# Gate and up products of two feed-forwards as seven block products of half the rows and half the tokens

## The chip, the cores and the metric

The kernel runs on one core of one Trainium2 chip. The metric is the device time of one execution in microseconds (us). Three runs of the kernel before gave 1549.69, 1547.15 and 1549.71 us, with a median of 1549.69. The engines are named TensorE (PE in the rows), VectorE (DVE), ScalarE (ACT), GpSimd (POOL) and SyncE (SP), which here only issues the transfers of weights.

## The reference, cut to what matters

Two transformer blocks follow each other on 512 tokens of width 1024. The first block has a feed-forward, a mixer (attention and pooling) and a second feed-forward; the change concerns its two feed-forwards. All arithmetic is float32.

```python
def rmsnorm(x, g):
    xf = x.astype(jnp.float32)
    y = xf * lax.rsqrt(jnp.mean(xf * xf, axis=-1, keepdims=True) + EPS)
    return (y * g.astype(jnp.float32)).astype(x.dtype)

def swiglu_ffn(x, w_gate, w_up, w_down):          # 1024 -> 2816 -> 1024
    return (jax.nn.silu(x @ w_gate) * (x @ w_up)) @ w_down

def first_block(x, ...):
    x = x + 0.5 * swiglu_ffn(rmsnorm(x, ffn1_norm[l]), ffn1_w_gate[l], ffn1_w_up[l], ffn1_w_down[l])
    x = x + hybrid_mixer(rmsnorm(x, mix_norm[l]), w_in[l], ...)
    x = x + 0.5 * swiglu_ffn(rmsnorm(x, ffn2_norm[l]), ffn2_w_gate[l], ffn2_w_up[l], ffn2_w_down[l])
    return rmsnorm(x, final_norm[l])
...
    x = second_block(x, ...)
```

## The kernel before

Activations lie transposed in SBUF: a tile is 128 features by 512 tokens, and x has eight of them (KD = 8, S = 512, H2 = 256). Every float32 product is made of three products on TensorE in a shorter format (fp32r). Each operand is split into a high part and the remainder: `split` rounds on ScalarE (`whi`, `xh`) and subtracts on VectorE (`wlo`, `xl`), and `mm3` adds high times high, high times low and low times high in one PSUM bank.

A feed-forward (`ffn`) takes the 2816 inner columns in three chunks of 8, 8 and 6 tiles of 128 (`FF1_CHUNKS`). For a pair, which is one tile of gate and one of up, `fgroup` makes 8 x 3 matmuls of 512 columns for gate and as many for up. The normalising factor of a token (`rsb`) is applied afterwards: VectorE multiplies both results by it out of PSUM, ScalarE makes silu of gate, GpSimd multiplies by up, and `split` makes the two parts of the inner activation (tiles `hh` and `hl` in the arena; a1f and a1r, or a2f and a2r, in the rows). After the pairs of a chunk come eight groups of down products, each added to X by VectorE.

Weights come in pieces of 1024 columns of 128 partitions (512 KB) by SyncE's queue into the ring `wraw` (three buffers), and `w_pump` splits each into the rings `whi` and `wlo` (four), two pieces ahead of their use (`SPLIT_AHEAD`).

Before the first feed-forward, `first_norm` transposes x in eight steps, splits it with its gain into `xh` and `xl`, copies it to X, and sums its squares (`sq` on ScalarE, `acc` on GpSimd). The second feed-forward's operands are prepared by `prep_sq` as the mixer's last products arrive. Small rows (gains, biases) are loaded by GpSimd's queue in the first microseconds (tile `rows`), and the mixer's Toeplitz table (`toeplitz`, held in XT) beside the first feed-forward.

The order of the instructions on each engine is written by a planner. Class `Program` collects all operations with a price for each (`cost`: by engine, columns, and whether PSUM is read; 2.11 ns a column + 147 ns for a tensor_tensor on GpSimd, 1.041 + 69 on VectorE with two operands) and a delay for a signal between engines; `issue` tries several sweeps, keeps the order that ends first, and issues it as a fixed order for each engine. Engines then wait for each other through semaphores only. There are two plannings: the first feed-forward and the mixer (arena a1), then the second feed-forward and the second block (arena a2). All recorded instructions have the line of that issue, so a row is told apart by its tiles.

Of the kernel before, what the change touches and what calls it, by code (L numbers as in the profile page):

```python
# [24 lines left out]
R_BUFS = 3  # L25
SPLIT_AHEAD = 2
ARENA = (5500, 16050)
# [250 lines left out]
class Arena:  # L278
# [13 lines left out]
    def tile(self, shape, dt=F32):  # L292
        n = math.prod(shape[1:])
        whole, at = self.whole[dt], self.at[dt]
        assert at + n <= whole.shape[1], (shape, dt, at)
        ap = whole[:shape[0], at:at + n]
        self.at[dt] += n
# [17 lines left out]
class Kern:  # L315
# [6 lines left out]
    def mm(self, out, lhsT, rhs, start=True, stop=True):  # L322
        self.pe.matmul(out, lhsT=lhsT, rhs=rhs, start=start, stop=stop)
# [107 lines left out]
    def w_init(self, pool):  # L431
        self.L = self.plan()
        self.raw = [pool.tile([P, 1024], F32, name=f"wraw{i}") for i in range(R_BUFS)]
        self.wh = [pool.tile([P, 1024], F32R, name=f"whi{i}") for i in range(W_BUFS)]
        self.wl = [pool.tile([P, 1024], F32R, name=f"wlo{i}") for i in range(W_BUFS)]
        self.w_dma = self.w_split = self.w_cur = 0
# [11 lines left out]
    def w_pump(self, upto):  # L448
        while self.w_split < min(upto + 1, len(self.L)):
            i = self.w_split  # L450
            self.w_load(i + R_BUFS)
            m = self.L[i][2] * self.L[i][3]
            step = m // 2 if i < 2 else m
            for c in range(0, m, step):
                c = slice(c, c + step)
                self.split(self.wh[i % W_BUFS][:, c], self.wl[i % W_BUFS][:, c], self.raw[i % R_BUFS][:, c])
            self.w_split += 1
            self.w_load(self.w_split + R_BUFS)

    def W(self, key, ahead=SPLIT_AHEAD):  # L460
        i = self.w_cur
        assert self.L[i][0] == key, (self.L[i][0], key)
        self.w_pump(i + ahead)
        self.w_cur += 1
        return self.w_view(self.wh[i % W_BUFS], i), self.w_view(self.wl[i % W_BUFS], i)


    def mm3(self, ps, ah, al, bh, bl, start, stop):
        self.mm(ps, ah, bh, start, False)
        self.mm(ps, ah, bl, False, False)  # L470
        self.mm(ps, al, bh, False, stop)
# [9 lines left out]
    def fgroups(self, bs, ws, xs, cols=slice(0, S)):  # L481

        n = len(xs)
        for k in range(n):
            for b, (wh, wl) in zip(bs, ws):
                self.mm3(b, wh[:, k, :], wl[:, k, :], xs[k][0][:, cols], xs[k][1][:, cols], k == 0, k == n - 1)

# [42 lines left out]
    def prep_sq(self, m, gcol):  # L530
        self.split(*self.xs[m], self.X[:, m, :], gcol)
        self.sq_acc(m, self.acc, self.X[:, m, :])
# [88 lines left out]
    def first_norm(self):  # L621
# [7 lines left out]
        self.w_pump(1)  # L629
# [780 lines left out]
```

## Time and profile before

| | |
|---|---|
| median of three runs | 1549.69 us |
| the profiled execution's own time | 1547.03 us |
| its span, first to last instruction | 1545.2 us |
| mean granted TensorE clock | 0.996 |
| TensorE busy | 1525.7 us (99%) |
| VectorE busy | 824.6 us (53%) |
| ScalarE busy | 648.4 us (42%) |
| GpSimd busy | 297.7 us (19%) |

A busy time is the time in which an engine has an instruction under way; the chain is the work that ended last, followed back from the end of the program. The rows that follow come from this one execution. A row of the timeline with xN stands for N like instructions in a row, with their time together.

### The profile page before, as it was taken

How to read it: one execution, taken by the hardware profiler on the slowest of the kernel's cores; microseconds unless marked ns; L12 is line 12 of the kernel's file. 1: busy time of each engine (PE TensorE's matmuls, PEld its weight loads, DVE VectorE, ACT ScalarE, POOL GpSimd, SP SyncE). 2: the span in 40 equal slices, each digit the busy share in tenths (PEclk: the TensorE clock that was granted, in tenths of full speed). 3: DMA queues.
4: the chain of work that ended last, by engine and by line, in shares of the span. 5: the costliest groups of instructions: out<-in, count | busy, mean ns of one | idle time of the engine just before them, and what ended most of it. 6: DMA issues, size and time to landing. Idle time of an engine off the chain costs nothing.

```text
span 1545.2 us, 18001 instructions
## 1 busy us (share of the span) xinstructions
PE 1525.7 (99%) x6931; PEld 1235.2 (80%) x6931; DVE 824.6 (53%) x1284; ACT 648.4 (42%) x1063; POOL 297.7 (19%) x290
## 2 busy tenths in 40 slices
PE   9999999999999999999999999999999999999997
PEld 7888888788877788888888887677788888888886
DVE  6443443336588884433443467998568524344345
ACT  6322232234367663312322275776555634233232
POOL 5120120212243321101200146331016000000002
PEclk9999999999999999999999999999999999999999
DMA  6333333533311133333433233121221332333321
GB/s 192 96 99 95 96 103 96 114 94 111 96 55 41 55 110 96 95 96 96 113 96 95 79 99 102 42 82 49 90 69 45 123 93 95 96 95 97 95 95 55
DMA packets 226757, 140.68 MB, mean 91 GB/s; under 512 B 5340, under 2 KB 212800, under 8 KB 226672
## 3 DMA queue, kind: packets, MB, share of 16 engines
q1 hardware_dynamic: 224832, 136.33, 30.1%
q0 software_dynamic: 1824, 3.21, 1.0%
q8 instruction: 54, 0.88, 0.2%
q14 instruction: 31, 0.25, 0.1%
q10 hardware_dynamic: 16, 0.00, 0.0%
HBM read 137.23 MB, written 2.29 MB: 90 GB/s over the span
## 4 chain that ended last, share of the span: by engine, by line
PE 92%; DVE 6%; ACT 1%; POOL 0%; issue 0%; DMA 0%; SPq 0%; DVEq 0%; POOLq 0%; ACTq 0%
PE bank L232 92%; DVE a2f L232 1%; DVE wlo L232 1%; ACT a2f L232 1%; DVE X L232 1%; DVE a2r L232 0%; DVE XT L232 0%; DVE xl L232 0%; DVE a1r L232 0%; DVE sq L232 0%; DMA XT<-x 0%; DVE cv L232 0%; POOL a2f L232 0%; DVE acc L232 0%; POOL acc L232 0%
## 5 line engine op out<-in xcount | busy, mean ns | idle before, releaser
L232 DVE TENSOR_TENSOR wlo<-wraw,whi 128x1024 fp32r<-128x1024 f32 (+2 forms) x258 | 325.2, 1262 | 417.8 <-ACT whi L232 352.9
L232 ACT ACTIVATE whi<-wraw 128x1024 fp32r<-128x1024 f32 (+2 forms) x258 | 267.5, 1039 | 518.8 <-PE bank L232 498.5
L232 PE MATMUL bank<-xl,whi 128*128 128x512 f32 (+1 forms) x1272 | 463.5, 384 | 2.5 <-DVE xl L232 2.5
L232 PE MATMUL bank<-xh,whi 128*128 128x512 f32 (+1 forms) x1272 | 462.6, 385 | 1.8 <-DVE a1r L232 1.0
L232 PE MATMUL bank<-xh,wlo 128*128 128x512 f32 (+1 forms) x1272 | 458.2, 383 | 0.0
L232 PEld LDWEIGHTS bank<-xl,whi 128*128 128x128 f32 x1272 | 239.4, 189 | 50.0 <-DVE xl L232 2.9
L232 PEld LDWEIGHTS bank<-xh,whi 128*128 128x128 f32 x1272 | 238.9, 189 | 49.7 <-issue 2.2
L232 PEld LDWEIGHTS bank<-xh,wlo 128*128 128x128 f32 x1272 | 239.1, 189 | 46.5 <-issue 1.9
L232 PE MATMUL bank<-whi,a2r 128*128 128x512 f32 (+1 forms) x528 | 155.6, 388 | 0.0
L232 PE MATMUL bank<-a1r,whi 128*128 128x512 f32 x480 | 151.2, 400 | 0.0
L232 PE MATMUL bank<-a2r,whi 128*128 128x512 f32 x416 | 130.0, 397 | 0.0
L232 POOL TENSOR_TENSOR a1f<-a1f 128x512 f32<-128x512 f32 x40 | 59.5, 1487 | 317.1 <-DVE a1f L232 311.6
L232 PEld LDWEIGHTS bank<-whi,a2r 128*128 128x128 f32 x528 | 98.2, 188 | 21.0
L232 POOL TENSOR_TENSOR a2f<-a2f 128x512 f32<-128x512 f32 x38 | 56.4, 1484 | 303.5 <-DVE a2f L232 252.3
L232 PEld LDWEIGHTS bank<-a1r,whi 128*128 128x128 f32 x480 | 89.7, 188 | 22.1 <-issue 0.9
L232 PE MATMUL bank<-wlo,a2r 128*128 128x512 f32 (+1 forms) x264 | 95.0, 389 | 0.0
L232 PEld LDWEIGHTS bank<-a2r,whi 128*128 128x128 f32 x416 | 77.3, 187 | 19.0 <-issue 0.7
L232 PE MATMUL bank<-a1r,wlo 128*128 128x512 f32 x240 | 91.1, 399 | 0.0
L232 ACT ACTIVATE a2r<-a2f 128x512 fp32r<-128x512 f32 (+3 forms) x83 | 51.0, 620 | 93.3 <-POOL a2f L232 55.3
L232 DVE TENSOR_TENSOR a2r<-a2f,a2r 128x512 fp32r<-128x512 f32 (+2 forms) x81 | 54.8, 680 | 49.7 <-ACT a2r L232 48.9
L232 PE MATMUL bank<-a2r,wlo 128*128 128x512 f32 x208 | 79.4, 397 | 0.0
L232 POOL TENSOR_TENSOR X<-X,a2f 128x512 f32<-128x512 f32 (+1 forms) x9 | 10.7, 1210 | 337.6 <-ACT a2f L232 337.6
(246 smaller groups left out, 1586.0 us busy)
## 6 DMA issues: line engine op xcount, KB each, us to landing
wraw<-ffn_w_gate SPq DMA_DIRECT2D x43, 512.0 KB, 3.8
wraw<-ffn_w_up SPq DMA_DIRECT2D x43, 512.0 KB, 3.8
wraw<-w_in SPq DMA_DIRECT2D x40, 512.0 KB, 3.9
wraw<-ffn_w_down SPq DMA_DIRECT2D x32, 512.0 KB, 3.9
wraw<-w_up SPq DMA_DIRECT2D x32, 512.0 KB, 4.0
wraw<-w_down SPq DMA_DIRECT2D x32, 512.0 KB, 3.6
wraw<-w_out SPq DMA_DIRECT2D x16, 512.0 KB, 3.5
wraw<-ffn_w_down SPq DMA_DIRECT2D x16, 384.0 KB, 3.4
```

The lines of the kernel that those rows point to most:

```text
L232: op.fn(*op.a, **op.k)
```

## The change

Two adjacent tiles of 128 columns, gate G and up U, over the 1024 rows of x form two by two blocks if the 1024 rows are halved (k tiles 0 to 3 and 4 to 7), and so does x, if the tokens are halved as well. The product needs eight block products in the plain way, which are the two groups of 24 matmuls before; the new `ffn` makes it of seven, each over four k steps and 256 tokens (`half_product`: 12 matmuls of 256 columns). The seven weights of a pair are three blocks, A11 and A12 (the two halves of gate) and A22 (the second half of up), and four sums S1 to S4 of blocks, made by GpSimd in the tiles sum0 and sum1; the seven operands of x are three blocks (11, 21, 22) and four differences (T1 to T4), made once for each feed-forward by `prep7` (ScalarE scales, VectorE and GpSimd subtract, and both parts are split). Weights are handled in units: `U` lists four for a pair (A11 and A12, S1 and S2, S3 and S4, A22) and one for a down group, and `W4` hands out a pair's four.

The seven results are combined while they are still in PSUM, partly by letting one bank accumulate two products and partly by VectorE (six additions or products of 256 columns out of PSUM, one of 256 from SBUF). The multiplication of up by `rsb` moves from VectorE to GpSimd. Scratch of the feed-forward moves into XT, so the Toeplitz table is loaded at the start of the mixer instead (`tape_out` and `toeplitz`). The second feed-forward moves to the first planning. The raw ring gets a fourth buffer. Of the diff, the new code is shown; what it takes the place of stands in the listing above.

```diff
--- before
+++ after
-R_BUFS = 3
+R_BUFS = 4
 SPLIT_AHEAD = 2
-ARENA = (5500, 16050)
+ARENA = (5640, 16050)
...
-        self.wh = [pool.tile([P, 1024], F32R, name=f"whi{i}") for i in range(W_BUFS)]
-        self.wl = [pool.tile([P, 1024], F32R, name=f"wlo{i}") for i in range(W_BUFS)]
-        self.w_dma = self.w_split = self.w_cur = 0
+        self.ring = [(pool.tile([P, 1024], F32R, name=f"whi{i}"), pool.tile([P, 1024], F32R, name=f"wlo{i}"))
+                     for i in range(W_BUFS)]
+        self.w_dma = self.w_made = self.w_cur = 0
+        self.U, self.at_unit = [], {}
+        for i, (key, _, _, _) in enumerate(self.L):
+            if key[1] == "u":
+                continue
+            self.at_unit[key] = len(self.U)
+            self.U += [(i, j) for j in range(4)] if key[1] == "g" else [(i, None)]
+        self.made = {}
+        self.sums = [pool.tile([P, 1024], F32, name=f"sum{q}") for q in range(2)]
...
+        while self.w_made < min(upto + 1, len(self.U)):
+            j = self.w_made
+            i, part = self.U[j]
+            h, l = buf = self.ring.pop(0)
+            self.ring.append(buf)
+            self.made[j] = buf
+            g = self.raw[i % R_BUFS]
+            if part is None:
+                self.w_load(i + 1)
+                m = self.L[i][2] * self.L[i][3]
+                self.split(h[:, :m], l[:, :m], g[:, :m])
+                self.w_load(i + 1 + R_BUFS)
+            else:
+                self.w_load(i + 2)
+                u = self.raw[(i + 1) % R_BUFS]
+                lo, hi = slice(0, S), slice(S, 2 * S)
+                if part == 0:
+                    for c in (lo, hi) if j < 4 else (slice(0, 2 * S),):
+                        self.split(h[:, c], l[:, c], g[:, c])
+                elif part == 3:
+                    self.split(h[:, lo], l[:, lo], u[:, hi])
+                    self.w_load(i + 2 + R_BUFS)
+                else:
+                    s12, s34 = self.sums
+                    if part == 1:
+                        self.tt(s12[:, lo], u[:, lo], u[:, hi], ALU.add, self.po)
+                        self.tt(s12[:, hi], s12[:, lo], g[:, lo], ALU.subtract, self.po)
+                        self.split(h, l, s12)
+                    else:
+                        self.tt(s34[:, lo], g[:, lo], u[:, lo], ALU.subtract, self.po)
+                        self.tt(s34[:, hi], g[:, hi], s12[:, hi], ALU.subtract, self.po)
+                        self.split(h, l, s34)
+            self.w_made += 1
...
+    def W4(self, key):
+        j = self.w_cur
+        assert self.at_unit[key] == j, (key, j)
+        self.w_pump(j + 3)
+        self.w_cur += 4
+        out = {}
+        for part, names in enumerate((("A11", "A12"), ("S1", "S2"), ("S3", "S4"), ("A22",))):
+            buf = self.made.pop(j + part)
+            for q, nm in enumerate(names):
+                out[nm] = tuple(t[:, q * S:(q + 1) * S].rearrange("p (k c) -> p k c", k=4) for t in buf)
+        return out
...
+    def half_product(self, ps, w, xs, start, stop):
+        wh, wl = w
+        for k in range(4):
+            self.mm3(ps, wh[:, k, :], wl[:, k, :], *xs[k], start and k == 0, stop and k == 3, skip_group_check=True)
...
+    def prep7(self, m, src, g):
+        hi, lo = self.mem7[m % 4]
+        st = self.first[m % 4]
+        b11, b12, t1 = (st[:, i * H2:(i + 1) * H2] for i in range(3))
+        if m < 4:
+            self.act(st[:, :2 * H2], src, AF.Copy, scale=g)
+            self.split(hi[:, :H2], lo[:, :H2], b11)
+            self.tt(t1, b12, b11, ALU.subtract, self.po)
+            self.split(hi[:, H2:2 * H2], lo[:, H2:2 * H2], t1)
+        else:
+            st = self.second.next()
+            b21, b22, t2, t3, t4 = (st[:, i * H2:(i + 1) * H2] for i in range(5))
+            self.act(st[:, :2 * H2], src, AF.Copy, scale=g)
+            self.split(hi[:, 2 * H2:4 * H2], lo[:, 2 * H2:4 * H2], st[:, :2 * H2])
+            self.tt(t2, b22, t1, ALU.subtract)
+            self.tt(t3, b22, b12, ALU.subtract, self.po)
+            self.tt(t4, b21, t2, ALU.subtract)
+            self.split(hi[:, 4 * H2:], lo[:, 4 * H2:], st[:, 2 * H2:])
+    def prep7_sq(self, m, gcol):
+        self.prep7(m, self.X[:, m, :], gcol)
         self.sq_acc(m, self.acc, self.X[:, m, :])
...
-        self.w_pump(1)
+        self.w_pump(3)
         for m in range(KD):
             b = tb.next()
             self.turn(b, [self.XT[:, t, m * P:(m + 1) * P] for t in range(NT)])
-            self.split(*self.xs[m], b, self.col("g1", m))
+            self.prep7(m, b, self.col("g1", m))
...
+    def toeplitz(self):
         self.T = te = self.XT[:].rearrange("p t d -> p (t d)").rearrange("p (h c) -> p h c", h=8)
...
+        low = self.XT[:].rearrange("p t d -> p (t d)")
+        at = [0]
+        def T(shape):
+            n = math.prod(shape[1:])
+            ap = low[:shape[0], at[0]:at[0] + n]
+            at[0] += n
+            return ap if len(shape) == 2 else ap.rearrange("p (a b) -> p a b", a=shape[1])
+        hh, hl = (self.mem.tile([P, 8, S], F32R, at=4096 * i) for i in range(2))
+        ga, ua = Rot([T([P, S]) for _ in range(2)]), Rot([T([P, S]) for _ in range(2)])
+        s1s = Rot([T([P, H2]) for _ in range(2)])
+        self.mmb = Rot(self.B)
+        x7, t0, t1 = self.x7, slice(0, H2), slice(H2, S)
+        for ci, (c0, n) in enumerate(FF1_CHUNKS):
+            for m in range(n):
+                j = self.w_cur
+                w = self.W4((tag, "g", c0 + m))
+                a, b, c = (self.bank()[:, :H2] for _ in range(3))
+                g, u, s1 = ga.next(), ua.next(), s1s.next()
+                self.half_product(a, w["A11"], x7["11"], True, True)
+                self.act(s1, a, AF.Copy)
+                self.half_product(c, w["S1"], x7["T1"], True, True)
+                self.half_product(b, w["S2"], x7["T2"], True, True)
+                self.tt(g[:, t1], b, s1, ALU.add)
+                self.half_product(a, w["A12"], x7["21"], False, True)
+                self.w_pump(j + 5)
+                self.half_product(b, w["S3"], x7["T3"], False, True)
+                self.tt(u[:, t1], b, s1, ALU.add)
+                self.tt(u[:, t1], c, u[:, t1], ALU.add)
+                self.half_product(c, w["S4"], x7["22"], False, True)
+                self.w_pump(j + 6)
+                self.half_product(b, w["A22"], x7["T4"], False, True)
+                if ci == 0 and m == 0:
+                    self.norm()
+                    self.prog.table(SILU)
+                self.tt(g[:, t0], a, self.rsb[:, t0], ALU.mult)
+                self.tt(g[:, t1], c, g[:, t1], ALU.add)
+                self.tt(g[:, t1], g[:, t1], self.rsb[:, t1], ALU.mult)
+                self.tt(u[:, t0], b, s1, ALU.add)
+                self.act(g, g, AF.Silu)
+                self.tt(u, u, self.rsb, ALU.mult, self.po)
+                self.tt(u, u, g, ALU.mult, self.po)
+                self.split(hh[:, m, :], hl[:, m, :], u)
...
+            self.toeplitz()
...
         k.mem = Arena(pool, *ARENA, "a1")
+        k.seven_init()
         k.first_norm()
-        k.ffn("f1", lambda m: k.prep_sq(m, k.col("gm", m)), [k.late_cols, k.toeplitz])
-        k.mixer1(lambda m: k.prep_sq(m, k.col("g2", m)))
+        k.ffn("f1", lambda m: k.prep_sq(m, k.col("gm", m)), [k.late_cols, k.tape_out])
+        k.mixer1(lambda m: k.prep7_sq(m, k.col("g2", m)))
+        k.ffn("f2", k.prep_final)
     with tc.tile_pool(name="m2", bufs=1) as pool:
         k.mem = Arena(pool, *ARENA2, "a2")
-        k.ffn("f2", k.prep_final)
         k.block2()
...
-    nc = bacc.Bacc("TRN2", target_bir_lowering=False, num_devices=1)
+    nc = bacc.Bacc("TRN2", target_bir_lowering=False, num_devices=1, dynamic_dma_scratch_size=4096)
```

GpSimd, from the end of the squares' sum (acc) in the first chunk on; before, the row of six is the products u times g of the first six pairs, and rows, hm2 are small loads:

```order
L232 TENSOR_TENSOR acc_99<-acc_99,sq0_102 128x512
L232 DMA rows_91<-q_norm 1x16x4 x2
L232 DMA rows_91<-k_norm 1x16x4 x2
L232 DMA hm2_89<-k_hm2 128x2
L232 TENSOR_TENSOR a1f_107<-a1f_107 128x512 x6
L232 DMA a1f_107<-k_anti 128x128
```

GpSimd after the change, in the same chunk (XT times rsb is up times the factor, XT from XT is u times g, sum0 and sum1 are the four sums, wraw the raw weights):

```order
L232 TENSOR_TENSOR XT_87<-XT_87,rsb_101 128x512
L232 TENSOR_TENSOR sum0_84<-wraw1_73 128x512
L232 TENSOR_TENSOR XT_87<-XT_87 128x512
L232 TENSOR_TENSOR sum0_84<-sum0_84,wraw0_72 128x512
L232 TENSOR_TENSOR XT_87<-XT_87,rsb_101 128x512
L232 TENSOR_TENSOR sum1_85<-wraw0_72,wraw1_73 128x512
L232 TENSOR_TENSOR sum1_85<-wraw0_72,sum0_84 128x512
L232 TENSOR_TENSOR XT_87<-XT_87 128x512
L232 TENSOR_TENSOR sum0_84<-wraw3_75 128x512
L232 TENSOR_TENSOR sum0_84<-sum0_84,wraw2_74 128x512
L232 TENSOR_TENSOR sum1_85<-wraw2_74,wraw3_75 128x512
```

Where one add for a pair stood, six stand, and each sum is placed between the steps of an earlier pair's u.

VectorE in the first chunk before, two pairs (a1f from bank and rsb is gate or up times the factor, a1r is the low part of the inner activation):

```order
L232 TENSOR_TENSOR a1f_107<-bank5_66,rsb_98 128x512
L232 TENSOR_TENSOR wlo0_79<-wraw1_73,whi0_75 128x1024
L232 TENSOR_TENSOR a1f_107<-bank6_67,rsb_98 128x512
L232 TENSOR_TENSOR wlo1_80<-wraw2_74,whi1_76 128x1024
L232 TENSOR_SCALAR a1f_107<-a1f_107 8x256
L232 TENSOR_TENSOR a1r_108<-a1f_107,a1r_108 128x512
L232 TENSOR_TENSOR a1f_107<-bank7_68,rsb_98 128x512
L232 TENSOR_TENSOR wlo2_81<-wraw0_72,whi2_77 128x1024
L232 TENSOR_TENSOR a1f_107<-bank0_61,rsb_98 128x512
L232 TENSOR_TENSOR wlo3_82<-wraw1_73,whi3_78 128x1024
L232 TENSOR_TENSOR a1r_108<-a1f_107,a1r_108 128x512
```

VectorE after the change, one pair in the same chunk:

```order
L232 TENSOR_TENSOR wlo2_81<-sum1_85,whi2_80 128x1024
L232 TENSOR_TENSOR XT_87<-bank4_65,XT_87 128x256
L232 TENSOR_TENSOR wlo3_83<-wraw1_73,whi3_82 128x512
L232 TENSOR_TENSOR XT_87<-bank1_62,XT_87 128x256
L232 TENSOR_TENSOR wlo1_79<-sum0_84,whi1_78 128x1024
L232 TENSOR_TENSOR wlo0_77<-wraw2_74,whi0_76 128x1024
L232 TENSOR_TENSOR XT_87<-bank4_65,XT_87 128x256
L232 TENSOR_TENSOR XT_87<-bank5_66,XT_87 128x256
L232 TENSOR_TENSOR XT_87<-bank3_64,rsb_101 128x256
L232 TENSOR_TENSOR a1r_111<-XT_87,a1r_111 128x512
L232 TENSOR_TENSOR XT_87<-bank5_66,XT_87 128x256
L232 TENSOR_TENSOR XT_87<-XT_87,rsb_101 128x256
```

Five differences and products from SBUF operands stand here for a pair where three stood, and two of the weights' differences read a sum that GpSimd writes.

## Rows read from the trace of the kernel before

**Rows 1.** The page: engine totals (share of span, instructions); chain's shares.

```profile
PE 1525.7 (99%) x6931; PEld 1235.2 (80%) x6931; DVE 824.6 (53%) x1284; ACT 648.4 (42%) x1063; POOL 297.7 (19%) x290
...
PE 92%; DVE 6%; ACT 1%; POOL 0%; issue 0%; DMA 0%; SPq 0%; DVEq 0%; POOLq 0%; ACTq 0%
```

**Rows 2.** Windows: stretch, us, busy us (x) of PE, PEld, DVE, ACT, POOL, clock, DMA, GB/s.

```profile
12.00:99.60 87.60, 87.60 (x393) 72.42 (x392) 49.95 (x53) 38.95 (x54) 27.53 (x23) 1.00 0.42 119
99.60:144.00 44.40, 44.40 (x192) 35.73 (x191) 15.59 (x18) 9.24 (x10) 2.22 (x1) 1.00 0.32 95
144.00:232.00 88.00, 88.00 (x390) 72.76 (x389) 35.10 (x42) 26.43 (x34) 12.16 (x10) 1.00 0.34 99
...
277.00:343.00 66.00, 66.00 (x292) 53.59 (x291) 25.22 (x32) 18.54 (x24) 12.18 (x16) 1.00 0.46 106
560.40:648.00 87.60, 87.60 (x387) 72.45 (x386) 46.06 (x51) 32.35 (x41) 16.48 (x11) 1.00 0.33 96
```

**Rows 3.** Timeline of TensorE (start, length, instruction), with 512 and with 256 columns.

```profile
180.18 0.39 PE L232 MATMUL bank<-xl,whi 128*128 128x512 f32 x1
...
190.83 0.39 PE L232 MATMUL bank<-xh,wlo 128*128 128x512 f32 x1
...
1192.11 0.29 PE L232 MATMUL bank<-xl,whi 128*128 128x256 f32 x1
...
1197.03 0.40 PE L232 MATMUL bank<-xl,whi 128*128 128x512 f32 x1
```

**Rows 4.** Instructions grouped by form, 144 to 232 us: busy us, mean ns, idle before.

```profile
L232 DVE TENSOR_TENSOR wlo<-wraw,whi 128x1024 fp32r<-128x1024 f32 x16 | 19.6, 1224 | 24.4 <-ACT whi L232 17.8 <-ACT a1r L232 5.1 <-PE bank L232 1.5
...
L232 DVE TENSOR_TENSOR a1r<-a1f,a1r 128x512 fp32r<-128x512 f32 x7 | 4.8, 690 | 10.1 <-ACT a1r L232 10.1
...
L232 POOL TENSOR_TENSOR a1f<-a1f 128x512 f32<-128x512 f32 x7 | 10.8, 1543 | 112.5 <-DVE a1f L232 112.5
...
L232 ACT ACTIVATE whi<-wraw 128x1024 fp32r<-128x1024 f32 x17 | 18.0, 1061 | 40.7 <-PE bank L232 36.6 <-issue 4.0
```

**Rows 5.** The same view, 377 to 560, 0 to 30, and 926 to 1545 us.

```profile
L232 DVE TENSOR_TENSOR a1r<-bank,a1r 128x256 fp32r<-128x256 f32 x8 | 3.4, 422 | 1.8 <-ACT a1r L232 1.8
...
L232 DVE SCALAR_TENSOR_TENSOR xl<-bank,cols,xh 128x512 fp32r<-128x512 f32 x8 | 5.9, 744 | 2.0 <-ACT xh L232 2.0
...
L232 POOL TENSOR_TENSOR a2f<-a2f,rsb 128x512 f32<-128x512 f32 x2 | 2.1, 1084 | 0.4 <-DVE rsb L232 0.4
...
L232 POOL TENSOR_TENSOR X<-X,a2f 128x256 f32<-128x256 f32 x2 | 1.4, 722 | 3.6 <-ACT a2f L232 3.6
```

**Rows 6.** Timeline, VectorE beside GpSimd, at 225 and at 594 us.

```profile
225.64 1.22 DVE L232 TENSOR_TENSOR wlo<-wraw,whi 128x1024 fp32r<-128x1024 f32 x1
...
225.86 2.14 POOL L232 TENSOR_TENSOR a1f<-a1f 128x512 f32<-128x512 f32 x1 [12.05 <-DVE a1f L232]
...
594.69 2.34 DVE L232 TENSOR_TENSOR wlo<-wraw,whi 128x1024 fp32r<-128x1024 f32 x1 [0.17 <-ACT whi L232]
...
594.66 1.29 POOL L232 TENSOR_TENSOR a2f<-a2f 128x512 f32<-128x512 f32 x1 [5.55 <-ACT whi L232]
```

**Rows 7.** Timeline, the same engines where the mixer ends, 555 to 567 us.

```profile
555.64 0.74 DVE L232 SCALAR_TENSOR_TENSOR xl<-X,cols,xh 128x512 fp32r<-128x512 f32 x1
...
558.66 0.68 DVE L232 TENSOR_TENSOR X<-bank,X 128x512 f32<-128x512 f32 x1
559.26 1.19 DVE L232 SCALAR_TENSOR_TENSOR xl<-X,cols,xh 128x512 fp32r<-128x512 f32 x1
...
560.97 1.19 DVE L232 SCALAR_TENSOR_TENSOR xl<-X,cols,xh 128x512 fp32r<-128x512 f32 x1
...
556.89 9.84 POOL L232 TENSOR_TENSOR acc<-acc,sq 128x512 f32<-128x512 f32 x6 [1.20 <-ACT sq L232]
```

**Rows 8.** Timeline at the start: one small load on GpSimd; VectorE's first preparation.

```profile
2.38 0.52 POOL L232 DMA_DIRECT2D rows<-ffn_norm  x1
...
5.76 0.75 DVE L232 SCALAR_TENSOR_TENSOR xl<-bank,cols,xh 128x512 fp32r<-128x512 f32 x1 [1.60 <-ACT xh L232]
```

## What the change will do to the time

> **What bounds the kernel now.** I read the engine totals and the chain of waits first, then one window per stage, then prices, then the places where VectorE and GpSimd meet. TensorE is busy 99% of the span and holds 92% of the chain; VectorE is busy 53%, GpSimd 19% [rows 1]. So a change can gain only through TensorE's time, and it loses wherever another engine makes TensorE wait. In the stages touched, TensorE is busy for the whole of each window at a granted clock of 1.00 (the 2.4 GHz level): 12.0 to 99.6 us is the first chunk of the first feed-forward's gate and up products (eight pairs of tiles), 144 to 232 the second, 277 to 343 the third (six pairs), 560.4 to 648.0 the first chunk of the second feed-forward [rows 2]. VectorE and GpSimd together are busy 35.10 + 12.16 = 47 us of 88 in the second chunk, 77 of 87.6 in the first: the first has the least room.
>
> **TensorE's part.** A pair is 48 matmuls of 512 columns before, 84 of 256 after. From 180.18 to 190.83 stand 47 starts: 226.6 ns each, 10.88 us a pair. Of 256 columns, 41 starts fill 1192.11 to 1197.03: 120 ns, 10.08 us a pair [rows 3]. The saving is 0.80 us a pair, 35 us over 44 pairs, if nothing else limits. The products fall by an eighth, their time by 7% only, since the shorter matmul costs 53% of the longer. The Trainium skill ("TensorE: Matmul & The Clock Gate", section "Wait — 56ns, not 53.3ns?") gives a start-to-start time of the columns over 2.4 GHz plus about 2.5 ns; by it the pair would go from 10.36 to 9.17 us and the saving would be 52 us; the rows show more at both sizes, and the rows decide.
>
> **The price of the sums.** Prices [rows 4, 5]: VectorE 1.224 us for a 1024-wide difference, 0.69 for 512 from SBUF, 0.42 for 256, 0.75 for a scalar_tensor_tensor of 512; 768 I put between 512 and 1024, at 0.96. ScalarE 1.06 for 1024. GpSimd: its 512-wide adds average 1.54 us, and 1.29 where nothing else runs beside them (594.66, [rows 6]); there are 1.08 us ones as well, which is the low end of my bounds; for 256 wide 0.72.
> Per pair the change takes from VectorE two 1024-wide differences, one 512 and two products from PSUM, and gives it three 1024-wide differences, two of 512, one of 256 and six of 256 from PSUM. GpSimd goes from one add to six (four sums of weights, u times the norm factor, u times g). ScalarE goes to about 5.4 us a pair (3.5 x 1.06 for weights, 0.6 twice for silu and h as over half of 1.06, 0.42 for the copy, taken as on VectorE), well under 10; I put it at nothing, hidden by TensorE.
>
> **What the rows say of two engines at once.** At 594.66 a GpSimd add runs 1.29 us and a VectorE difference started at 594.69 lasts 2.34 instead of 1.22; at 225.64 VectorE is first, lasts 1.22, and the GpSimd add lasts 2.14 [rows 6]. Both read two operands from SBUF. At 556.89 GpSimd makes six adds in 9.84 us with VectorE's differences in between; these start 1.71 us apart (559.26, 560.97), where 1.29 + 0.74 would be 2.03; VectorE's addition from PSUM at 558.66 keeps its 0.68 [rows 7]. So instructions with two SBUF operands take turns, each handover saves 0.16 us (half of 0.32), and operations that read PSUM are not touched. The planner that sets the order knows nothing of this: its prices have no other engine in them.
> The Trainium skill ("SBUF — State Buffer", section "Who interferes with whom") calls this an exclusive lock on a shared port pair, and says that a VectorE instruction with two SBUF inputs contends with GpSimd's reads; the rows agree with the turns, and differ by the 0.16 us. By it nothing would be saved at a handover; what the time would be then stands among the rivals.
> A pair needs in turns GpSimd 6 x 1.29 = 7.7 and VectorE 3 x 1.224 + 2 x 0.69 + 0.42 = 5.5: 13.2 us; with twelve handovers, 13.2 - 1.9 = 11.3. TensorE needs 10.08, and needed 10.88. The turns are the new bound by a small margin, and where no sums can be made ahead the kernel is slower than before.
>
> **First chunk, first feed-forward.** The new order has 63 GpSimd instructions that take turns there (32 sums, 16 on u, 7 of the squares, 8 of 256 in the new preparation) and 80 of VectorE (27 of 1024, 23 of 512, 2 of 0.75, 4 of 768, 24 of 256). GpSimd 55 x 1.29 + 8 x 0.72 = 76.7; VectorE 33.0 + 15.9 + 1.5 + 3.8 + 10.1 = 64.3; sum 141.0; less 126 handovers x 0.16 = 20.2: 120.8 us. The first may start at about 6.3 (the first preparation is at 5.76 now, [rows 8]; a copy on ScalarE now comes ahead of it), so the last ends at 127.1. Of that, some 7 us lie behind TensorE's last gate or up product (the last pair's u chain, about 5, and the first down products that need only earlier pairs, 2). So that product ends no earlier than 120.1, against 99.6: +20.5 if the turns never pause, +25 if they idle 4%. I take +23. The 15 or so loads of small rows, 0.52 us each on GpSimd's queue [rows 8], now stand between the sums: 8 us of GpSimd in which VectorE can take its turns, so nothing by itself, and up to +8 if they fall when the turns wait for GpSimd.
>
> **First chunk, second feed-forward.** 51 + 8 on GpSimd: 71.6. VectorE, with fewer halves of weights: 61.7. Less 118 x 0.16 = 18.9: 114.4. It may start at about 554, as the mixer's first outputs arrive (the preparation at 555.64 now, [rows 7]). End 668.4, less 7: 661.4 against 648.0, +13.4; with the same idling, +15.6.
>
> **Later chunks.** During the down products (99.6 to 144) GpSimd is busy 2 of 44 us and VectorE 16 [rows 2], so the sums of the next two pairs can be made then. That leaves for eight pairs 40 x 1.29 + 8 x 5.47 = 95.4, less 80 x 0.16: 82.6; TensorE 80.6. I take 83.6 against 87.0: -3.4, twice. For six pairs 28 x 1.29 + 32.8 - 9.0 = 59.9, TensorE 60.5; I take 63 against 65.3: -2.3, twice. Together -11.4.
>
> **At nothing:** the Toeplitz loads, which move from beside the feed-forward to the mixer's start: the 96 products of V (22 us at 0.227) cover them, and up to +10 if they don't. The weights' transfers: same bytes, DMA share 0.34 [rows 2]. The second block, which loses only the feed-forward at its planning boundary: between -3 and +3.
>
> **The sum:** 23 + 15.6 - 11.4 = +27 on the profiled run, 1547.0 us (span 1545.2): 1574. The runs shown lie at 1547.2 to 1549.7, so I do not add for the median. With GpSimd's low price, 1.08, the first chunks lose 11 less each: 1552. With idling of 10%, 12 more: 1590. Likeliest's own range 1556 to 1592.
>
> **Rivals.**
> *Faster:* TensorE stays the bound, because the turns are shorter than I think: most GpSimd adds fall where VectorE is waiting for ScalarE or PSUM, or cost 1.08. For it: VectorE idles 24 us ahead of the wlo group in the second chunk [rows 4]. Against: those waits vanish as the engine fills. Then -35, plus a later start: the seven operands of four k steps cost VectorE 4 x 3.3 = 13.2 us against 8 x 0.75 = 6.0, with weights in between, some +14 and, behind the mixer, +10: -11, so 1536. The point where it decides: a turn sum of a pair under 10.1 us.
> *Gain and loss cancel,* within 0.2% (3 us): the first chunks lose half of what I say and the later ones gain 6 each. 1548.
> *Slower still:* in the later chunks the sums are not made ahead, because the ring of four split buffers is full while the down products run; then every pair goes at the turns' pace, 11.3 against 10.88, +12 over the 28 later pairs in place of -11, and with the first chunks at their upper ends (25 + 18): +55, 1602. For it: the rings of raw weights and of split weights have four buffers each, and a down product takes one of each. Against: the new order shows sums of three pairs ahead of the first product on u.
> *No overlap at handovers:* 141.0 + 6.3 - 7 - 99.6 = +40.7 in the one first chunk, 133.3 + 554 - 7 - 648 = +32.3 in the other, 95.4 against 87.0 and 68.9 against 65.3 twice each in the later ones, +24: +97, 1644. The 0.16 us of [rows 7] speaks against it.
>
> **How the numbers follow.** Forecast 0.50, faster rival 0.23, cancel 0.09, slower still 0.15, no overlap 0.03. 0.2% is about what a measurement of this kernel can tell from no change. Faster: 0.23 + 0.02 of the cancelling case; same 0.07; slower 0.68. The range goes from 1532 (the faster rival with less of a late start) to 1604 (the slower one). What lies outside are the far ends of these cases, about 0.15.
>
> **What would show it.** Right: TensorE shows gaps in 12 to 125 us, released by VectorE's wlo or GpSimd's sums; wlo's mean there is 1.7 us or more and the sums' mean about as much; the gate and up products of the first chunk end near 122, those of the second chunk take near 84 us. Wrong: TensorE 99% busy in the first chunk (then the faster rival); wlo at 1.3 us beside busy GpSimd (then no turns); pairs of the later chunks at 11 us or more (then the slower one). The gap-free pace must be 120 ns; if the 256-column products run at 0.11 us, the gain is larger by about 37 us.

## The result and the profile after

The changed kernel takes 1633.26 us (median of four runs, 1632.71 to 1634.13), the kernel before 1549.70: a ratio of 1.0544, 95% interval 1.0526 to 1.0562. The direction was forecast; the size, +84 us against +27, was not, and it lies outside the range.

The totals and the chain of the page, which answer to [rows 1]:

```profile
span 1631.6 us, 22156 instructions
...
PE 1533.0 (94%) x8515; PEld 1301.8 (80%) x8515; DVE 1097.7 (67%) x1623; ACT 743.6 (46%) x1226; POOL 673.0 (41%) x526
...
PE 71%; DVE 20%; issue 3%; POOL 3%; ACT 3%; DVEq 0%; ACTq 0%; POOLq 0%
```

TensorE has seven more busy microseconds although it has less to multiply, some of them at the lower clock (below); VectorE's part of the chain has gone from 6% to 20%.

The windows that answer to [rows 2] (same columns), cut where the last gate or up product of each chunk ends:

```profile
11.20:132.00 120.80, 98.56 (x691) 91.84 (x692) 107.41 (x122) 58.46 (x87) 98.09 (x69) 0.87 0.33 90
132.00:172.40 40.40, 40.40 (x177) 32.62 (x177) 16.83 (x19) 10.12 (x11) 10.88 (x8) 1.00 0.34 98
172.40:271.50 99.10, 89.12 (x691) 85.37 (x690) 78.78 (x96) 39.61 (x54) 66.23 (x44) 0.98 0.31 89
...
602.00:721.50 119.50, 97.78 (x686) 90.42 (x685) 103.65 (x121) 54.40 (x78) 83.56 (x53) 0.90 0.26 74
```

In both first chunks VectorE and GpSimd are together busy for more than 187 us of 120, and TensorE stands still for 22 of them. What it waits for in the first (waits in 11.2 to 132 us: total, times, longest; the longest four) are weights' differences, and then the prepared operands xl and a1r:

```profile
PE bank L232 <- DVE wlo L232: 7.9, 11, 1.2
PE bank L232 <- DVE xl L232: 4.6, 2, 3.1
PE bank L232 <- DVE a1r L232: 3.6, 2, 1.8
PE bank L232 <- DVE XT L232: 2.7, 3, 1.5
```

In the second chunk it stands still for 10 of 99 (the same view, 172.4 to 271.5):

```profile
PE bank L232 <- DVE wlo L232: 7.7, 7, 2.4
PE bank L232 <- DVE XT L232: 1.7, 2, 0.9
PE bank L232 <- ACT whi L232: 0.3, 1, 0.3
```

What makes VectorE late is seen in the timeline at 200 us; [rows 6] had the like in two places, and here it is the rule:

```profile
202.03 2.32 DVE L232 TENSOR_TENSOR wlo<-sum,whi 128x1024 fp32r<-128x1024 f32 x1
204.27 2.30 DVE L232 TENSOR_TENSOR wlo<-wraw,whi 128x1024 fp32r<-128x1024 f32 x1
206.50 1.07 DVE L232 TENSOR_TENSOR XT<-bank,XT 128x256 f32<-128x256 f32 x3
...
201.53 1.74 POOL L232 TENSOR_TENSOR sum<-wraw,wraw 128x512 f32<-128x512 f32 x1
203.22 2.27 POOL L232 TENSOR_TENSOR sum<-wraw,sum 128x512 f32<-128x512 f32 x1
```

Each of the two engines takes up to 2.3 us for what alone takes 1.22 or 1.29; the three instructions that read PSUM keep 0.4 each. By form in the window 172.4 to 271.5, against [rows 4]:

```profile
L232 DVE TENSOR_TENSOR wlo<-sum,whi 128x1024 fp32r<-128x1024 f32 x14 | 22.7, 1627 | 2.1 <-ACT whi L232 1.8
L232 DVE TENSOR_TENSOR wlo<-wraw,whi 128x1024 fp32r<-128x1024 f32 x10 | 18.1, 1807 | 2.5 <-ACT whi L232 2.4
L232 DVE TENSOR_TENSOR XT<-bank,XT 128x256 f32<-128x256 f32 x39 | 15.6, 417 | 13.3 <-PE bank L232 12.1 <-POOL XT L232 0.8
...
L232 POOL TENSOR_TENSOR XT<-XT,rsb 128x512 f32<-128x512 f32 x8 | 14.6, 1828 | 9.3 <-DVE XT L232 9.3
L232 POOL TENSOR_TENSOR sum<-wraw,sum 128x512 f32<-128x512 f32 x7 | 13.2, 1889 | 0.0
```

Where the time went, by the end of the last gate or up product of each chunk (us; the end of the span in the last column). The first two rows are the two kernels; the rest are experiments told below:

| | f1, 1st | 2nd | 3rd | f2, 1st | 2nd | 3rd | end |
|---|---|---|---|---|---|---|---|
| before | 99.6 | 232 | 343 | 648.0 | 780 | 889.7 | 1545.2 |
| after | 131.9 | 271.4 | 382.9 | 721.4 | 861.2 | 974.9 | 1631.6 |
| no sums | 111.2 | 236.0 | 343.8 | 659.8 | 788.6 | 894.2 | 1550.1 |
| no sums, no differences of x | 101.4 | 227.7 | 335.2 | 639.0 | 763.2 | 868.5 | 1524.8 |

From row to row of the first two: +32.3 in the first chunk, +7.1 and +0.5 in the next two, +33.5 in the mixer and the first chunk of the second feed-forward, +7.8 and +4.0 in its others, +1.2 after it.

### The profile page after: what moved, and what is told of

Read it like the earlier page. It is cut to its first block, busy times and chain, and to the rows that moved or that the text cites. A ratio compares the mean times of both kernels' runs of the same rounds, so it can differ in the third digit from the quotient of the medians.

```text
span 1631.6 us, 22156 instructions
## 1 busy us (share of the span) xinstructions
PE 1533.0 (94%) x8515; PEld 1301.8 (80%) x8515; DVE 1097.7 (67%) x1623; ACT 743.6 (46%) x1226; POOL 673.0 (41%) x526
## 3 DMA queue, kind: packets, MB, share of 16 engines
q8 instruction: 66, 1.08, 0.3%
## 4 chain that ended last, share of the span: by engine, by line
PE 71%; DVE 20%; issue 3%; POOL 3%; ACT 3%; DVEq 0%; ACTq 0%; POOLq 0%
PE bank L232 71%; DVE wlo L232 9%; DVE a1r L232 2%; DVE XT L232 2%; DVE xl L232 1%; DVE a2f L232 1%; DVE a1f L232 1%; DVE X L232 1%; POOL sum L232 1%; ACT whi L232 1%; DVE sq L232 1%; POOL a2f L232 1%; ACT a2f L232 1%; POOL XT L232 1%; POOL a1f L232 0%
## 5 line engine op out<-in xcount | busy, mean ns | idle before, releaser
L232 PE MATMUL bank<-a1r,whi 128*128 128x256 f32 (+1 forms) x2064 | 513.4, 333 | 9.9 <-DVE a1r L232 9.8
L232 PE MATMUL bank<-xh,wlo 128*128 128x256 f32 (+1 forms) x1184 | 385.0, 336 | 44.4 <-DVE wlo L232 44.0
L232 PEld LDWEIGHTS bank<-a1r,whi 128*128 128x128 f32 x2064 | 357.2, 193 | 48.5 <-DVE a1r L232 13.2
L232 PE MATMUL bank<-xh,whi 128*128 128x256 f32 (+1 forms) x1184 | 377.2, 333 | 13.0 <-DVE XT L232 7.8
L232 PE MATMUL bank<-xl,whi 128*128 128x256 f32 (+1 forms) x1184 | 379.5, 331 | 8.8 <-DVE xl L232 8.6
L232 PE MATMUL bank<-a1r,wlo 128*128 128x256 f32 (+1 forms) x1032 | 322.2, 331 | 1.8 <-DVE wlo L232 1.7
L232 PEld LDWEIGHTS bank<-xh,wlo 128*128 128x128 f32 x1184 | 227.7, 194 | 75.3 <-DVE wlo L232 55.9
L232 PEld LDWEIGHTS bank<-a1r,wlo 128*128 128x128 f32 x1032 | 194.3, 192 | 22.7 <-DVE wlo L232 3.9
L232 DVE TENSOR_TENSOR wlo<-sum,whi 128x1024 fp32r<-128x1024 f32 x88 | 138.3, 1574 | 22.5 <-ACT whi L232 11.8
L232 ACT ACTIVATE whi<-sum 128x1024 fp32r<-128x1024 f32 x88 | 93.1, 1058 | 127.4 <-PE bank L232 112.9
L232 DVE TENSOR_TENSOR XT<-bank,XT 128x256 f32<-128x256 f32 x236 | 96.0, 417 | 66.9 <-PE bank L232 61.5
```

Source lines behind the costliest of these rows:

```text
L232: op.fn(*op.a, **op.k)
```

## Are the sums dear because they take turns, or because others wait for them?

```diff
 # no sums
-                        self.split(h, l, s12)          # and the two additions ahead of it
+                        self.split(h, l, u)
-                        self.split(h, l, s34)          # and the two additions ahead of it
+                        self.split(h, l, g)
 # sums that nobody reads: the four additions stay
-                        self.split(h, l, s12)
+                        self.split(h, l, u)
-                        self.split(h, l, s34)
+                        self.split(h, l, g)
```

> Leaves out the four sums of weights of every pair: the units S1/S2 and S3/S4 are split from the raw up and gate pieces instead, so the products have other weights. Theory A (VectorE's and GpSimd's two-operand instructions take turns, and the sum of the turns sets the pace): the turns of a pair fall from 13.2 to 8.0 us, under TensorE's 10.08, so later chunks take 81 us for eight pairs and the time is 1535 to 1565. Theory B (the pace is set by waits around the sums: one pair of sum tiles, written by GpSimd, read by ScalarE and VectorE, before the next can be written): the same. Theory C (VectorE's own added instructions, combination and preparation, are too many, whoever makes the sums): stays above 1600.

> GpSimd makes the four sums of every pair as before, but nothing reads them: the units S1/S2 and S3/S4 are split from the raw up and gate pieces (other weights). Theory A: the turns are all still there, 13.2 us a pair less handovers, so the time stays within 25 us of 1633, and the wlo differences beside the sums still last 1.6 us or more. Theory B: nobody waits for a sum, so the time is within 15 us of that of the kernel without sums (about 1550). In between, both have a part, in the ratio of the two distances.

Without sums 1549.97 us, ratio to before 1.0014 (1.0004 to 1.0024). With sums that nobody reads 1638.37, ratio 1.0584 (1.0563 to 1.0605): no faster than the changed kernel, though nothing waits for a sum. So the price, 83 us in the changed kernel and 88 here, is not in the waits for sums or their tiles; it is in what the additions do to VectorE. Both kernels have the same 1623 VectorE instructions, form by form, and with the additions beside them these keep VectorE busy 100 us longer (the pages, first without sums, then with sums that nobody reads):

```profile
PE 1505.5 (97%) x8515; PEld 1287.6 (83%) x8515; DVE 995.6 (64%) x1623; ACT 739.3 (48%) x1226; POOL 372.9 (24%) x350
...
PE 1535.5 (94%) x8515; PEld 1305.1 (80%) x8515; DVE 1095.9 (67%) x1623; ACT 741.9 (45%) x1226; POOL 661.0 (40%) x526
```

TensorE's waits for wlo over all six chunks grow with it (14 to 895 us of the first kernel, then 14 to 981 of the second):

```profile
PE bank L232 <- DVE wlo L232: 6.2, 13, 1.4
...
PE bank L232 <- DVE wlo L232: 54.0, 54, 3.7
```

In the second chunk (148 to 236 us, then 173.6 to 275.7) the differences themselves:

```profile
L232 DVE TENSOR_TENSOR wlo<-wraw,whi 128x1024 fp32r<-128x1024 f32 x24 | 30.2, 1262 | 10.0 <-ACT whi L232 7.1 <-PE bank L232 2.4
```

```profile
L232 DVE TENSOR_TENSOR wlo<-wraw,whi 128x1024 fp32r<-128x1024 f32 x24 | 40.6, 1702 | 6.9 <-ACT whi L232 4.1 <-PE bank L232 2.3 <-issue 0.2
```

The same 24 instructions take 1.26 us each in the one and 1.70 in the other. Theory B falls, and so does theory C, which had the kernel without sums above 1600. What the additions do to GpSimd's own queue, where u's two products stand behind them, is not separated here; TensorE has no wait for GpSimd among its longest, but GpSimd's part of the chain is 3% after the change and 2% without sums. The first kernel says a second thing too: even with free sums the change gains nothing, so my faster rival (1536) left something out, of which the last experiment of the next section finds the larger part.

```diff
 # four sum tiles: successive pairs use two pairs of tiles in turn
-                    s12, s34 = self.sums
+                    s12, s34 = self.sums if (i // 2) % 2 == 0 else self.sums2
```

> The sums of successive pairs go to two pairs of tiles in turn (the second pair lies in the arena's space that the preparation of the operands has left), so that GpSimd can make a pair's sums while VectorE still reads the last ones. Theory A alone: between 1615 and 1635, since the turns are as many. Theory B: the idle time between turns in the four later chunks (13 us in 99 of the second) goes, 1580 or less.

1629.92 us, ratio 1.0529 (1.0513 to 1.0544), 3 us less than the changed kernel. A second pair of tiles is worth next to nothing, as theory A had it. But the second chunk shows more. Added up from the timeline between its first and its last gate or up product, the turns fill 82.3 us there, against 86.7 in the changed kernel, since more sums are made ahead; 17.8 us instead of 13.4 are idle, and the chunk takes 100.1 us both times. So the idle time between turns has another cause than the tiles, and in the later chunks the sum of the turns does not set the pace alone.

## Shortening the turns

```diff
 # sums by VectorE: in all four additions
-                        self.tt(s12[:, lo], u[:, lo], u[:, hi], ALU.add, self.po)
+                        self.tt(s12[:, lo], u[:, lo], u[:, hi], ALU.add)
 # shifted operands (n = 4 for 16 bytes, n = 2 for 8); ua and sums alike
+        self.raw = [pool.tile([P, 1032], ...)[:, n * (i % 2):n * (i % 2) + 1024] for i in range(R_BUFS)]
```

> The four sums of a pair are made by VectorE (0.69 us each) in place of GpSimd (1.29). Theory A (turns): the first chunk's 137 us of turns lose 32 x 0.6 = 19, so each first chunk ends 15 to 20 us earlier; in later chunks the turns of a pair fall from 13.2 to 10.8. VectorE's own time of a pair becomes 5.5 + 2.8 + 2.5 (from PSUM) = 10.8 plus its waits for two GpSimd turns, so a pair takes 11.5 or so: some 1585 in all. Theory C (VectorE has too many instructions of its own): slower than 1633.

> Same instructions in the same order; the odd raw buffers, the sum tiles and the two tiles for up start 16 bytes later, so that five of a pair's six GpSimd additions read operands that do not start at the same place within 32 bytes. In the kernel before, GpSimd's 512-wide additions took 1.08 us in such cases and 1.29 otherwise. Theory A: 5 x 0.21 = 1.05 us less of turns a pair; where turns are nearly always under way (both first chunks) 8 us each, in the later chunks somewhat less than 1.05 a pair: 1590 to 1605. Theory B: two of these additions lie in the loop around the sums, 0.4 us a pair: about 1615. If the position does not matter: 1633.

> As the kernel shifted by 16 bytes (whose additions still took 1.29 us), with 8 bytes, the distance of the two additions that took 1.08 us in the kernel before. Same instructions in the same order. If the distance matters, five of six additions take 0.2 us less where alone, and the time by theory A is 1595 to 1615; if those two were quick for another reason, 1633.

Sums by VectorE: 1586.12, ratio 1.0253 (1.0232 to 1.0273), 47 us faster than the changed kernel and in total as forecast, though not in each place: the first chunk of the first feed-forward ends 7 us earlier (124.8), not 15 to 20. VectorE does four more instructions a pair and the kernel gets faster, which speaks against theory C once more: the length of the turns counts, 0.69 us for 1.29.

The shift by 16 bytes: 1633.41, no change. By 8 bytes: 1604.25, ratio 1.0373 (1.0355 to 1.0390), 29 us faster, with the same instructions in the same order. The additions where VectorE leaves them alone (timeline of GpSimd), with 16 bytes:

```profile
154.31 1.28 POOL L232 TENSOR_TENSOR sum<-wraw,wraw 128x512 f32<-128x512 f32 x1
155.56 1.29 POOL L232 TENSOR_TENSOR sum<-wraw,sum 128x512 f32<-128x512 f32 x1
```

and with 8 bytes:

```profile
147.18 1.09 POOL L232 TENSOR_TENSOR sum<-wraw,wraw 128x512 f32<-128x512 f32 x1
148.23 1.08 POOL L232 TENSOR_TENSOR sum<-wraw,sum 128x512 f32<-128x512 f32 x1
```

My expectation on the 16 bytes was wrong. Over both feed-forwards the shortest of each of the five additions takes 1.08 to 1.09 us with 8 bytes; the sixth, both of whose operands lie in the same raw buffer and move together, keeps 1.28. So it is the distance between the two operands that counts here, not the place of either. A saving of 0.21 us in five additions of 44 pairs is 46 us at most; 29 came back, so about two thirds of a shorter turn reaches TensorE.

```diff
 # planner's prices while the two feed-forwards are recorded
-            return 2.11 * n + 147.0 if fn == "tensor_tensor" else 0.83 * n + 200.0
+            return (2.11 * n + 147.0) * 1.35 if fn == "tensor_tensor" else 0.83 * n + 200.0
-        return 1.041 * n + 69.0 + 61.0 * cols
+        return (1.041 * n + 69.0 + 61.0 * cols) * (1.35 if len(big) > 1 and not psum else 1.0)
```

> The planner's prices of GpSimd's additions and of VectorE's instructions with two SBUF operands are multiplied by 1.35 while the two feed-forwards are recorded, nearer to what the turns make of them; same instructions in another order. Theory A with a share for the order: the turns' idle 13 us of 99 in the second chunk fall to 5 or less, so the four later chunks gain 25 to 30 us: about 1605. If the order has no share: within 8 us of 1633.

1612.60, ratio 1.0424 (1.0403 to 1.0445): 21 us less by the order alone. The order has a share. But of the 21 us about 11 come from the mixer and the first chunk of the second feed-forward, and only 12 from the later chunks (the first chunk of the first feed-forward lost 4, ending at 136.2), so the place that I had named holds half of it. Nor did it come as I had named it: the turns' idle time in the second chunk did not fall to 5 us; it is 12 of 96, where the changed kernel has 13 of 100.

```diff
 # no sums, and no differences of x: T1 to T4 are neither made nor split
+        self.x7.update(T1=self.x7["11"], T2=self.x7["22"], T3=self.x7["21"], T4=self.x7["11"])
```

> On top of the kernel without sums, the four differences of x (T1 to T4) and their splits are left out, and the products read the blocks 11, 22, 21 and 11 in their place (other products). If the preparation of the operands is what makes the first chunks 18 us later than TensorE's own saving allows: 1515 to 1525. If it is the late start of the first pair (units of weights, gaps with TensorE at its lower clock): 1540 to 1550.

1526.77 us, ratio 0.9869 (0.9849 to 0.9889), 2 us above the range that I had for it: 23 us less than without sums alone, of which 10 by the first chunk's end and 12 in the mixer and the first chunk of the second feed-forward (the table above). The faster rival had 24 us for the late starts of both first chunks; they are 35, and the differences of x make 22 of these. The preparation's stretches in the changed kernel (windows):

```profile
14.00:38.00 24.00, 14.53 (x55) 11.90 (x54) 24.00 (x25) 12.71 (x23) 16.77 (x14) 0.50 0.29 74
604.00:620.00 16.00, 8.37 (x27) 5.90 (x26) 16.00 (x20) 9.33 (x18) 9.55 (x8) 0.57 0.00 0
```

VectorE is busy throughout, TensorE makes 55 matmuls in 24 us, and its granted clock is 0.50, the 1.2 GHz level, after the gaps that these waits leave; behind the mixer it falls from 1.00 (590 to 604 us) to 0.57 likewise.

## A version that beats both

The reasons say where seven products pay: where the turns have room and nothing is prepared ahead of them. In the next versions the first chunk of each feed-forward is as in the kernel before. Its split x stays in place, and three of the seven operands are halves of it; T1 to T4 are made during that chunk's down products. Only pairs of the later chunks use seven products: every second, two of three, or all. Shift by 8 bytes and prices as above; the sums' tiles lie in the arena.

```diff
+def seven(m):                                  # half: and m % 2 == 1; two of three: and (m - 8) % 3 != 0
+    return m >= 8
+    def make_t(self, k):                       # four times, in the first chunk's down products
+        lo, hi, t = self.scr.next()
+        for d, m in ((lo, k), (hi, k + 4)):
+            self.tt(d, self.xs[m][0].bitcast(F32), self.xs[m][1].bitcast(F32), ALU.add)
...
+        self.split(*self.tk[k], t)
...
+                if not seven(c0 + m):          # the pair as in the kernel before
 # in the last version also
-                        self.tt(s12[:, lo], u[:, lo], u[:, hi], ALU.add, self.po)
+                        self.tt(s12[:, lo], u[:, lo], u[:, hi], ALU.add)
```

> A version made from the reasons: the first chunk of each feed-forward stays plain (its operands as before); the four differences T1 to T4 are made from the split x during that chunk's down products, where the turns are nearly free; the blocks 11, 21, 22 are read from the split x itself; in the two later chunks every second pair uses seven products; operands 8 bytes apart; planner's prices of these instructions times 1.35. Theory A: the turns of two pairs are 12.2 + 4.2 us against 21 of TensorE, so TensorE stays busy, the first chunks cost nothing, and 14 pairs save 0.8 us each: 1536. If the differences or the mixed order cost as much as they save: 1547.

> The same, with two of three pairs in the later chunks as seven products (18 pairs). Theory A: turns (12.2 + 12.2 + 4.2) = 28.6 less handovers 26 against 31 us of TensorE for three pairs: nearly all of 18 x 0.8 = 14 is kept: 1533 to 1538.

> The same, with all 28 pairs of the later chunks as seven products. Theory A: turns of a pair 12.2 less 1.7 of handovers, 10.5, above TensorE's 10.08: the saving stops at the turns' pace, and at the 10% of idle turns that these chunks showed it is lost again: 1540 to 1550, slower than with two of three.

> The version with all 28 later pairs as seven products, and the first of the four sums (upper plus lower half of up, the one addition that still takes 1.29 us on GpSimd) made by VectorE in 0.69. Theory A: the turns of a pair fall from 10.5 to 9.9 us, under TensorE's 10.08, so TensorE's 10 us of waits for VectorE in the feed-forwards fall and the time is 1533 to 1537. If VectorE's own time (8.7 us of turns and 2.5 from PSUM, in order) is the bound there: 1541 to 1548.

| pairs with seven products | us | ratio to before (95%) |
|---|---|---|
| half of the later ones | 1538.98 | 0.9941 (0.9926 to 0.9956) |
| two of three | 1538.71 | 0.9942 (0.9926 to 0.9959) |
| all | 1541.09 | 0.9952 (0.9937 to 0.9967) |
| all, first sum by VectorE | 1536.97 | 0.9926 (0.9909 to 0.9943) |

All four are faster than the kernel before, by 0.5 to 0.7%, and than the changed kernel by 6%. Half of the pairs gave 8.8 us of the 11 that their products should save, and two of three no more (9 of 14). That "all" is behind "two of three" was expected, but the intervals overlap and it is not shown; nor is the last version's lead over the first two. TensorE's waits in 9 to 930 us tell the versions apart better. With every pair:

```profile
PE bank L237 <- DVE XT L237: 5.0, 11, 0.7
PE bank L237 <- DVE wlo L237: 3.6, 6, 1.4
```

With two of three, nothing waits for wlo or XT, and the longest wait is another:

```profile
PE bank L237 <- DVE a1r L237: 2.5, 2, 2.0
PE bank L237 <- DMA XT<-x: 1.0, 1, 1.0
```

With all, and the first sum by VectorE, what is left is 4.4 us for wlo and 2.7 for XT: the time came out at the edge of its range, but the expectation that these waits would mostly go was wrong.

## Why the prediction was wrong

*TensorE's part was right.* The kernel without sums and differences (the table's fourth row) shortens its four later chunks by 6.1, 3.5, 7.8 and 4.4 us against the first row, 21.8 together, where 28 pairs of 0.80 us are 22.4. In the two first chunks it is 1.8 us late and 1.2 early, where 6.4 early was due in each; what still holds them back there was not taken apart. So 20 us of my 35 is all that the products could bring in this form.

*The turns were right in kind and price.* From 11.2 to 132 us wlo's 1024-wide differences last 1.70 us on the average and the sums as much, as the prediction asked. (A pair has six VectorE instructions with two SBUF operands, as the prediction counts, not the five told with the change.) Adding up from the timeline the stretches of 6 to 132 us in which a two-operand instruction of either engine is under way, pauses of under 0.15 us included, gives 121.9 us; I had 120.8 for the whole chunk. The prices add to some 137 us by then, over 105 handovers: 0.14 us each, where I took 0.16 from [rows 7].

*The step that failed* is the one from the turns to the ends of the chunks: how much of them lies behind, how often they hand over, and how long they pause. Between the +27 forecast and the +86 of the two spans lie 59 us: 9 in the first chunk of the first feed-forward, 18 up to the end of that of the second, 31 in the later chunks, 1 behind them.

In the first chunk it is "some 7 us lie behind TensorE's last gate or up product". Some 4 did: 137 of the 141.0 us of prices stand ahead of it, and with 105 handovers in place of 126 these take 121.9 us, not 113.8 (120.8 less the 7); tail and handovers make about half of that each. With the 4 us in which no turn is under way the chunk ends at 131.9, not 122.6: +32.3, not +23. I had taken an estimate of the tail as a credit, without looking up in the new order what stands behind that product.

In the second feed-forward the same credits failed, and the idle share too: from 592 to 721.4 the turns fill 118.0 us (I had 114.4, less 7), with 98 handovers in place of 118, and 11.4 us are idle, not 2.2, nearly all of it after 625 us, when the preparation is over, as in the later chunks. +33.5 in place of +15.6.

*The later chunks*, "I take 83.6 against 87.0", failed mostly on idle turns. In the second chunk the turns fill 85.9 us (82.6 by my sum), but 13 of 99 are idle. I had added 1 us for that. In the forms above VectorE stands still for 12.1 us until TensorE has made the products that its additions from PSUM read; at each of TensorE's seven waits for wlo, 7.7 us together, VectorE is at work on the lengthened difference itself. Each engine thus waits for the other at another time. Four sum tiles show that it is not the tiles; another order took 12 us off these chunks and left the idle turns as they were. So what makes the turns idle stays open. 19.4 us for these four chunks in place of -11.4.

*The rest was right.* After the second feed-forward +1.2 us. The mixer, with the Toeplitz loads at its start, costs about 2 us at most: the second feed-forward's first product starts at 602.4 against 560.4, 42 later, where 39.9 had been lost by the end of the third chunk.

Of the rivals, "no overlap at handovers" (1644) came nearest in time, by chance. By the exclusive lock of the Trainium skill ("SBUF — State Buffer", section "Who interferes with whom") the 137 us of prices in the first chunk would fill 137 us; they took 121.9, since handovers overlap. "Slower still" (1602) had a better price for the later chunks, +12, but not its reason: six or seven sums of each later chunk, of the eight that I had taken, are made before its first product starts. The faster rival's case, TensorE as the bound, is what the kernel without sums shows, and it gives 1550, not 1536, since the late starts cost 35 us in the first chunks (11.6 and 11.0 late, where 6.4 early was due in each), not 24. One sum of the range was wrong by itself: 12 us more than 1574 is 1586, not 1590.

So of the 83.6 us: the sums cost 83.3 and the preparation's differences 23.2, against the 20 (0.9869 of 1547.1) that the products bring; the runs of before beside those were 2.6 us shorter, which is the rest. These shares hold the order too: the planner lays a new one for each of these kernels, and the order alone moved the time by 21 us above.

## What to carry to other kernels

Before trading matrix work for additions, add up the instructions of VectorE and GpSimd with two SBUF operands as if they were on one engine. Here that sum, 13.2 us a pair, passed TensorE's 10.08, and the kernel lost. The sum is only a lower bound: the turns stood idle for 12 to 14 us more in each later chunk. The engine with the shorter instruction is the better place for such an addition (0.69 us for 1.29 brought 47 us back). Bound the end of a stage by all of the shared work that the order puts ahead of its last product, and give no credit for a tail that has not been looked up. Use the cheaper products only where the shared time has room: here in the later chunks, with the operands prepared during the down products.

## What the runs showed that I had not expected

Where VectorE leaves them alone, GpSimd's additions of two 512-wide operands take 1.28 to 1.30 us, as they are and with one operand moved by 16 bytes, and 1.08 to 1.09 with one moved by 8 bytes; that alone moved the kernel by 29 us. VectorE and GpSimd, both with two operands in SBUF, hand over with 0.14 us of overlap on the average of the first chunk's 105 handovers. And TensorE's clock goes to the 1.2 GHz level in the preparation's gaps (0.50 in 14 to 38 us, 0.57 in 604 to 620), so that the matmuls that are left there also take longer: two of 256 columns start 0.22 us apart at 23 us, in place of 0.12 [rows 3].
